# Up-projection units multiplied in pairs, in runs of 32 products

## The chip, the cores and the metric

The kernel runs on one core of one Trainium2 chip. The metric is the time of one execution on the device in microseconds; before the change the median of three runs is 2297.98 us (2297.76 to 2298.06).

The engines are called here as the profile calls them: PE (TensorE, the matrix products, with PEld for its weight loads), DVE (VectorE), ACT (ScalarE), POOL (GpSimd) and SP (the queue from which most loads are started). Each works through its own list of instructions in the order in which the program wrote it, and they wait for each other by semaphores.

## The reference, cut to what matters

Two layers, each a mixer of four kinds of attention and a feed-forward stage, on 256 positions of width 2048, in float32. The change concerns the feed-forward stage:

```python
hin = _rms_norm(x, norm_mlp_pre[l])
u = hin @ mlp_w_up[l]                      # 2048 -> 2 * 5632
u_pad = jnp.pad(u, ((0, 0), (CONV_WIDTH - 1, 0), (0, 0)))
conv = mlp_conv_b[l] + mlp_conv_w[l][0] * u_pad[:, 0:s_len]
for tap in range(1, CONV_WIDTH):
    conv = conv + mlp_conv_w[l][tap] * u_pad[:, tap:tap + s_len]
gate, up = jnp.split(conv, 2, axis=-1)
y = (jax.nn.gelu(gate, approximate=True) * up) @ mlp_w_down[l]
x = x + _rms_norm(y, norm_mlp_post[l])
```

## The kernel before, in words

**Split numbers.** A float32 weight tile `raw` is split into `hi` (rounded to the format fp32r, an ACT copy, L193) and `lo` (the rest, a DVE subtraction, L196). The activations are split once per stage into 512 columns per block of 128 channels: 256 columns high part, 256 low part (tiles `HL0` to `HL3`). A *high product* multiplies a 128x128 piece of `hi` with all 512 columns; a *low product* multiplies a piece of `lo` with the 256 high columns only. Both add into one PSUM bank, 512 columns wide.

**Units and granules.** The up-projection of a layer has 88 units of 128 output channels, even ones of the gate, odd ones of the up half. A unit needs 16 high and 16 low products (one per block of 128 input channels, `KT` = 16). Its weights come in two granules of 128x1024, which are loaded, split and used one after the other. Loads, `hi` and `lo` each have a ring of six buffers (`RAW_BUFS`, `HL_BUFS`). Units 0 to 2 are worked on in `start_block`, together with the end of the stage before; units 3 to 87 are a loop over `w_unit`.

**Order of the work.** Everything is written out in a fixed order when the program is built. `w_unit` adds two parts, one for each granule. A part is `run_gran`:

```python
fill("v")
ready(g)
emit()
used(g)
fill("pe")
```

`fill("v")` takes each *chain* that is under way one step further; `ready(g)` writes the splits of granules up to five ahead of `g` (`LOOK`), as far as their buffers' last users have been marked by `used`; `emit` writes the products. In `mm_runs` the first granule of a unit does 8 high and then 8 low products, the second 8 low and then 8 high, so that over successive units runs of 16 high (L430) and 16 low (L435) alternate.

**The chain behind a unit** is `evac(i)` in `mlp`. Its steps, one for each `fill("v")`: an ACT copy of the bank's low columns (`u`, L1504); then on DVE five operations (add the high columns L1506, multiply by the row scale L1512, and the three taps of the convolution L1515 and L1518 twice); then, for a gate unit, the GELU on ACT (`gl`, L1524), for an up unit the product with the GELU of the unit before it on DVE (`y`, L1528). When all units are done, `out_units` multiplies `y` with the down-projection (L732 to L734); it first splits each `y` into two tiles `xs`, by an ACT copy (L704) and a DVE subtraction (L705).

Of the kernel before, what the change touches and what calls it, by code (L numbers as in the profile page):

```python
# [22 lines left out]
KT = D // 128  # L23
FF = 5632
NF = FF // 128
# [111 lines left out]
def hybrid_kernel(ctx, tc, a):  # L137
    nc = tc.nc
    V, SC, TE, GP = nc.vector, nc.scalar, nc.tensor, nc.gpsimd
# [3 lines left out]
    ps = ctx.enter_context(tc.tile_pool(name="ps", bufs=1, space=bass.MemoryType.PSUM))  # L143
# [6 lines left out]
    def take(kind):  # L150
        live[kind] += 1
        assert live[kind] <= cap[kind], kind
# [5 lines left out]
    def bank():  # L158
        take("ps")
        return ps.tile([128, 512], F32, tag="ps", name="bank", bufs=8)  # L160
# [4 lines left out]
    def gran(src, c0, n, whole=False):  # L165
        return Granule(src[:, c0:c0 + n], n, whole)

    def add(f, *gs):
        work.append((f, gs))
# [46 lines left out]
    def ready(g, look=LOOK):  # L216
        prep(g.idx + look)
        assert g.idx < state["gran"]

    def used(g):  # L220
        g.uses -= 1
# [5 lines left out]
    def launch(gen, cost=0.0):  # L227
        c = Chain(gen)
        budget[0] -= cost
        if c.kind is not None:  # L230
            active.append(c)
        return c

    def may(c):
        return (all(live[k] + n <= lim[k] for k, n in c.need.items())
                and (c.cond is None or c.cond()))

    def step(c):
        c.step()
        if c.kind is None:  # L240
            active.remove(c)

    def fill(kind):
        n = 0
        for c in list(active):
            if c.kind == kind and may(c):
                step(c)
                n += 1
        return n

    def start(gain):
        budget[0] = min(budget[0] + gain, 2.0)
        n = 0
        while budget[0] > 0:
            for i in range(min(3, len(queue))):
                cost, fn, cond = queue[i]
                if cond is None or cond():
                    c = Chain(fn())
                    if not may(c):
                        continue  # L260
                    del queue[i]
                    budget[0] -= cost
                    active.append(c)
                    if c.kind == "pe":
                        step(c)
                    n += 1
                    break
            else:
                break
        return n  # L270
# [9 lines left out]
    def room(kind, n=1):  # L280
        force(lambda: live[kind] + n <= cap[kind])
# [33 lines left out]
    HL = [None] * 4  # L315
# [52 lines left out]
    def hview(k):  # L368
        return HL[k // 4][:, k % 4, :256]
# [271 lines left out]
    def w_unit(src, evac, cost):  # L641
        u = src
        gs = [gran(u, 0, 1024), gran(u, 1024, 1024)]
        box = {}

        def part(h):
            def run():
                def emit():
                    if h == 0:
                        room("ps")  # L650
                        box["a"] = bank()
                    mm_runs(box["a"], gs[h], h)
                run_gran(gs[h], 2.56, emit)
                if h == 1:
                    launch(evac(box["a"]), cost)
            return run
        add(part(0), gs[0])
        add(part(1), gs[1])

    def x_units(srcs, width, evac, cost):  # L660
        box = {}
# [196 lines left out]
    def over():  # L858
        while ends:
            ends.pop()()  # L860
# [622 lines left out]
    def mlp(l):  # L1483
        st = {}

        def begin():
            over()
            es = ExitStack()
            mp = es.enter_context(tc.tile_pool(name=f"mlp{l}", bufs=1, reuse_waits="tile"))
            st["es"], st["mp"], st["done"] = es, mp, set()  # L1490
            st["cw"] = mp.tile([128, 2 * NF + 8, 4], F32, name="cw")[:, :2 * NF]
            GP.dma_start(out=st["cw"], in_=a["conv"][l])
            st["y"] = [mp.tile([128, 256], F32, name=f"y{j}") for j in range(NF)]
            on_rows[0] = lambda: None

        def evac(i):
            j, up = divmod(i, 2)

            def f(p, first=None):
                yield "v", dict(u=1)  # L1500
                mp = st["mp"]
                take("u")
                u = mp.tile([128, 256], F32, tag="u", name="u", bufs=4)
                SC.activation(u, p[:, 256:], AF.Copy)  # L1504
                yield "v"
                V.tensor_tensor(u, u, p[:, :256], op=OP.add)  # L1506
                drop("ps")
                if first is not None:
                    add_first(u, first)
                if not scaled[0]:  # L1510
                    yield "v", {}, is_scaled
                V.tensor_tensor(u, u, r2bc, op=OP.mult)  # L1512
                cv = mp.tile([128, 256], F32, tag="cv", name="cv", bufs=5)
                w = st["cw"][:, i]
                V.tensor_scalar(cv, u, w[:, 2:3], w[:, 3:4], op0=OP.mult, op1=OP.add)  # L1515
                for tap in (1, 0):
                    n = 2 - tap
                    V.scalar_tensor_tensor(cv[:, n:], u[:, :256 - n], w[:, tap:tap + 1], cv[:, n:], op0=OP.mult,  # L1518
                                           op1=OP.add)
                drop("u")  # L1520
                if not up:
                    yield "v"
                    g = mp.tile([128, 256], F32, tag="gl", name="gl", bufs=3)
                    SC.activation(g, cv, AF.Gelu_apprx_tanh)  # L1524
                    st["g", j] = g
                else:
                    yield "v", {}, lambda: ("g", j) in st
                    V.tensor_tensor(st["y"][j], st["g", j], cv, op=OP.mult)  # L1528
                    st["done"].add(j)
            return f  # L1530

        UP = a["w_up"]
        start_block(2 * l + 1, [UP[l, i] for i in range(3)], [evac(i) for i in range(3)], mgs)
        add(begin)
        for i in range(3, 2 * NF):
            w_unit(UP[l, i], evac(i), 0.0)
        out_units(2 * l + 1, lambda p_, k2: a["w_down"][l, p_, k2], NF, lambda k: st["y"][k],
                  lambda k: k in st["done"], mgs, tail_norm(mgs) if l < DEPTH - 1 else tail_out(mgs),
                  Left(lambda: st["mp"].tile([128, 256], F32R, tag="xs", name="xs", bufs=12), "xs"),
                  lambda: st["mp"].tile([128, 1024], F32, tag="gpost", name="gpost"), l == DEPTH - 1)  # L1540

        def end():
            live["xs"] = 0
            st["es"].close()
        add(lambda: ends.append(end))
# [3 lines left out]
    for l in range(DEPTH):  # L1549
        mixer(l)  # L1550
        mlp(l)
# [95 lines left out]
```

## Time and profile before

| what | value |
|---|---|
| median of three runs | 2297.98 us |
| the profiled execution | 2297.9 us |
| its span (first to last instruction) | 2296.1 us |
| PE busy in the span | 2282.3 us, 99% |
| DVE busy | 1686.8 us, 73% |
| ACT busy | 1176.4 us, 51% |
[...]
| DMA, mean | 191 GB/s |

The time of the profiled execution is 1.8 us longer than its span; this part lies outside the instructions. Busy shares are means over stages: the up-projection of layer 0 runs from 434 to 908 us of the span, that of layer 1 from 1575 to 2049 us, each followed by its down-projection. In the timeline view a row gives start, time from the first start to the last end of a merged group, engine, line, operation, tiles, count, and in brackets how long the engine sat idle just before and what ended that.

### The profile page before, as it was taken

What the parts mean: (1) busy time and instruction counts of PE and PEld (TensorE: products, weight loads), DVE (VectorE), ACT (ScalarE), POOL (GpSimd) and SP (SyncE); (2) the same over time, 40 slices, a digit from 0 to 9 for tenths busy, and PEclk for the clock granted to TensorE, in tenths of its full rate; (3) what the DMA queues carried; (4) which work ended last, traced back from release to release, by engine and by line L of the source; (5) the groups of instructions that cost most, each with busy time, mean ns of one, the idle gap of its engine ahead of it and who ended that gap; (6) DMA issues with size and microseconds to landing.
All of it is one profiled execution on the core that took longest, in us unless ns stands there. A gap on an engine that the chain in (4) does not pass through costs nothing.

```text
span 2296.1 us, 33239 instructions
## 1 busy us (share of the span) xinstructions
PE 2282.3 (99%) x12485; PEld 1967.3 (86%) x12485; DVE 1686.8 (73%) x2901; ACT 1176.4 (51%) x1927; POOL 50.0 (2%) x71
## 2 busy tenths in 40 slices
PE   9999999999999999999999999999999999999998
PEld 7888888888888888888888888888888888888887
DVE  6757666898888888565586576568988888885655
ACT  6454555654444444455464555656444444445543
POOL 1000000100000000000010000001000000000000
PEclk9999999999999999999999999999999999999999
DMA  8764556466565565656556645564665555655663
GB/s 280 250 220 148 155 174 202 157 205 201 185 190 189 190 189 187 200 184 212 175 194 234 211 143 173 170 195 160 210 193 192 190 187 189 190 191 195 202 195 115
DMA packets 122658, 437.56 MB, mean 191 GB/s; under 512 B 13888, under 2 KB 14016, under 8 KB 122496
## 3 DMA queue, kind: packets, MB, share of 16 engines
q1 hardware_dynamic: 120384, 429.40, 57.4%
q0 software_dynamic: 1824, 5.94, 1.0%
q8 instruction: 98, 1.61, 0.3%
q14 instruction: 64, 0.52, 0.1%
q10 hardware_dynamic: 288, 0.10, 0.0%
HBM read 433.28 MB, written 2.10 MB: 190 GB/s over the span
## 4 chain that ended last, share of the span: by engine, by line
PE 96%; ACT 1%; DVE 1%; issue 1%; DMA 0%; POOL 0%; SPq 0%; DVEq 0%; POOLq 0%; ACTq 0%
PE bank L430 36%; PE bank L435 19%; PE bank L734 9%; PE bank L733 9%; PE bank L732 9%; PE bank L684 2%; PE bank L686 2%; PE bank L685 2%; PE bank L1158 1%; PE bank L1080 1%; ACT hi L193 1%; PE bank L423 1%; PE bank L467 0%; DVE x L411 0%; ACT trash L397 0%
## 5 line engine op out<-in xcount | busy, mean ns | idle before, releaser
L196 DVE TENSOR_TENSOR lo<-raw,hi 128x1024 fp32r<-128x1024 f32 (+1 forms) x786 | 948.2, 1210 | 496.3 <-ACT hi L193 495.7
L193 ACT ACTIVATE hi<-raw 128x1024 fp32r<-128x1024 f32 (+1 forms) x786 | 815.6, 1046 | 425.0 <-PE bank L734 248.3
L430 PE MATMUL bank<-HL,hi 128*128 128x512 f32 x3648 | 880.4, 392 | 0.4 <-DVE u L1506 0.4
L430 PEld LDWEIGHTS bank<-HL,hi 128*128 128x128 f32 x3648 | 668.9, 188 | 131.2 <-issue 2.8
L435 PEld LDWEIGHTS bank<-HL,lo 128*128 128x128 f32 x3648 | 469.5, 191 | 21.5 <-DVE qk L950 1.6
L435 PE MATMUL bank<-HL,lo 128*128 128x256 f32 x3648 | 480.3, 283 | 0.0
L732 PE MATMUL bank<-hi,xs 128*128 128x512 f32 x960 | 374.8, 390 | 0.0
L734 PE MATMUL bank<-hi,xs 128*128 128x512 f32 x960 | 373.6, 389 | 0.0
L733 PE MATMUL bank<-lo,xs 128*128 128x512 f32 x960 | 373.5, 389 | 0.0
L734 PEld LDWEIGHTS bank<-hi,xs 128*128 128x128 f32 x960 | 180.2, 188 | 37.3
L733 PEld LDWEIGHTS bank<-lo,xs 128*128 128x128 f32 x960 | 180.3, 188 | 37.0
L732 PEld LDWEIGHTS bank<-hi,xs 128*128 128x128 f32 x960 | 180.3, 188 | 36.9
L1518 DVE SCALAR_TENSOR_TENSOR cv<-u,cw,cv 128x255 f32<-128x255 f32 x352 | 170.0, 483 | 12.6
L1504 ACT ACTIVATE u<-bank 128x256 f32<-128x256 f32 x176 | 66.7, 381 | 202.0 <-PE bank L430 201.9
L1524 ACT ACTIVATE gl<-cv 128x256 f32<-128x256 f32 x88 | 36.8, 418 | 222.2 <-DVE cv L1518 222.2
L684 PE MATMUL bank<-hi,HL 128*128 128x512 f32 (+1 forms) x256 | 96.7, 378 | 0.5 <-ACT r2bc L501 0.5
L686 PE MATMUL bank<-hi,HL 128*128 128x512 f32 (+1 forms) x256 | 93.4, 365 | 0.0
L685 PE MATMUL bank<-lo,HL 128*128 128x512 f32 (+1 forms) x256 | 93.4, 365 | 0.0
L1512 DVE TENSOR_TENSOR u<-u,r2bc 128x256 f32<-128x256 f32 x176 | 74.9, 426 | 5.8
L1515 DVE TENSOR_SCALAR cv<-u,cw 128x256 f32<-128x256 f32 x176 | 72.6, 412 | 6.4
L1506 DVE TENSOR_TENSOR u<-u,bank 128x256 f32<-128x256 f32 x176 | 73.0, 415 | 0.0
L705 DVE TENSOR_TENSOR xs<-y,xs 128x256 fp32r<-128x256 f32 x176 | 72.1, 417 | 0.0
(227 smaller groups left out, 1402.2 us busy)
## 6 DMA issues: line engine op xcount, KB each, us to landing
raw<-in_w_up SPq DMA_DIRECT2D x352, 512.0 KB, 4.3
raw<-in_w_down SPq DMA_DIRECT2D x176, 512.0 KB, 3.7
raw<-in_w_cols SPq DMA_DIRECT2D x122, 512.0 KB, 4.4
raw<-in_w_out SPq DMA_DIRECT2D x64, 512.0 KB, 4.3
raw<-in_w_v SPq DMA_DIRECT2D x48, 512.0 KB, 4.1
raw<-in_cmp SPq DMA_DIRECT2D x32, 512.0 KB, 4.6
gpost<-in_gpost POOLq DMA_DIRECT2D x8, 512.0 KB, 6.1
raw<-in_w_x SPq DMA_DIRECT2D x8, 408.0 KB, 4.7
```

Source lines behind the costliest of these rows:

```text
L193: SC.activation(g.hi[:, c0:c0 + n], g.raw[:, c0:c0 + n], AF.Copy)
L196: eng.tensor_tensor(g.lo[:, c0:c0 + n], g.raw[:, c0:c0 + n], g.hi[:, c0:c0 + n].bitcast(F32), op=OP.subtract)
L430: TE.matmul(o, lhsT=g.hi[:, k % 8 * 128:k % 8 * 128 + 128], rhs=HL[k // 4][:, k % 4, :], start=(k == 0), stop=(k == KT - 1))
L435: TE.matmul(o[:, :256], lhsT=g.lo[:, k % 8 * 128:k % 8 * 128 + 128], rhs=hview(k), start=False, stop=False)
L684: TE.matmul(o, lhsT=h, rhs=wh, start=(K == 0), stop=False)
L685: TE.matmul(o, lhsT=h, rhs=wl, start=False, stop=False)
L686: TE.matmul(o, lhsT=lo, rhs=wh, start=False, stop=(K == KT - 1))
L732: TE.matmul(o, lhsT=h_, rhs=wh, start=(k[1] == 0), stop=False)
L733: TE.matmul(o, lhsT=h_, rhs=wl, start=False, stop=False)
L734: TE.matmul(o, lhsT=l_, rhs=wh, start=False, stop=(k[1] == nk - 1))
L1512: V.tensor_tensor(u, u, r2bc, op=OP.mult)
L1518: V.scalar_tensor_tensor(cv[:, n:], u[:, :256 - n], w[:, tap:tap + 1], cv[:, n:], op0=OP.mult, op1=OP.add)
```

## The change

A new function `w_pair` takes two units at once, with two banks, and replaces the loop over `w_unit` for units 3 to 86 of each layer (42 pairs, an up unit first and a gate unit second; unit 87 is left to `w_unit`). Its four parts write: 16 high products of the first unit and one of the second (this one clears the second bank); 16 low products of the first unit; 16 low products of the second; 15 high products of the second. With the next pair's first part this gives runs of 32 high and 32 low products. The chain behind the first unit is launched after the second part, that behind the second unit after the fourth; `used` marks granules of the first unit after the second part and of the second unit after the fourth; `ready` is called in parts 1, 2 and 3.

```diff
+    def w_pair(srcs, evacs):
+        gs = [[gran(src, 0, 1024), gran(src, 1024, 1024)] for src in srcs]
+        acc = [None, None]
+
+        def his(i, k0, k1):
+            for k in range(k0, k1):
+                g = gs[i][k // 8]
+                TE.matmul(acc[i], lhsT=g.hi[:, k % 8 * 128:k % 8 * 128 + 128], rhs=HL[k // 4][:, k % 4, :],
+                          start=(k == 0), stop=(i == 1 and k == KT - 1))
+
+        def los(i):
+            for k in range(KT):
+                g = gs[i][k // 8]
+                TE.matmul(acc[i][:, :256], lhsT=g.lo[:, k % 8 * 128:k % 8 * 128 + 128], rhs=hview(k),
+                          start=False, stop=(i == 0 and k == KT - 1))
+
+        def part(n):
+            def run():
+                fill("v")
+                if n == 0:
+                    for g in (*gs[0], gs[1][0]):
+                        ready(g)
+                    room("ps", 2)
+                    acc[:] = bank(), bank()
+                    his(0, 0, KT)
+                    his(1, 0, 1)
+                elif n == 3:
+                    his(1, 1, KT)
+                else:
+                    ready(gs[n - 1][1])
+                    los(n - 1)
+                if n % 2:
+                    for g in gs[n // 2]:
+                        used(g)
+                fill("pe")
+                start((3.6, 1.5)[n in (1, 2)])
+                if n % 2:
+                    launch(evacs[n // 2](acc[n // 2]))
+            return run
+        for n, g in enumerate((gs[0][0], gs[0][1], gs[1][0], gs[1][1])):
+            add(part(n), g)
...
-        for i in range(3, 2 * NF):
+        for i in range(3, 2 * NF - 1, 2):
+            w_pair([UP[l, i], UP[l, i + 1]], [evac(i), evac(i + 1)])
+        for i in range(2 * NF - (2 * NF - 3) % 2, 2 * NF):
             w_unit(UP[l, i], evac(i), 0.0)
```

The order of instructions before and after, at the places on which the prediction rests. Lines below the new function move by 42: L1506 becomes L1548, L1518 becomes L1560, L1524 becomes L1566, L1528 becomes L1570, L705 becomes L747, L734 becomes L776; L193 and L196 stay.

ACT in the up-projection of layer 0, before the change. `gl_4728` is the GELU of a gate unit, `cv_4702` the result of its five DVE operations; `hi_4708` and `hi_4734` are the next two granules to be split.

```order
L193 ACTIVATE hi_4679<-raw_4538 128x1024
L193 ACTIVATE hi_4708<-raw_4568 128x1024
L1524 ACTIVATE gl_4728<-cv_4702 128x256
L1504 ACTIVATE u_4730<-bank_4683 128x256
L193 ACTIVATE hi_4734<-raw_4597 128x1024
L193 ACTIVATE hi_4763<-raw_4623 128x1024
```

And now; `gl_4724` and `cv_4704` belong to the gate unit, `hi_4730` and `hi_4736` are the next two granules.

```order
L193 ACTIVATE hi_4673<-raw_4496 128x1024
L193 ACTIVATE hi_4679<-raw_4562 128x1024
L1566 ACTIVATE gl_4724<-cv_4704 128x256
L1546 ACTIVATE u_4726<-bank_4683 128x256
L193 ACTIVATE hi_4730<-raw_4568 128x1024
L193 ACTIVATE hi_4736<-raw_4619 128x1024
```

DVE at the same place before the change: the five operations of the gate unit, and the `lo` splits after them.

```order
L196 TENSOR_TENSOR lo_4680<-raw_4538,hi_4679 128x1024
L1506 TENSOR_TENSOR u_4675<-u_4675,bank_4629 128x256
L1512 TENSOR_TENSOR u_4675<-u_4675,r2bc_72 128x256
L1515 TENSOR_SCALAR cv_4702<-u_4675,cw_4377 128x256
L1518 SCALAR_TENSOR_TENSOR cv_4702<-u_4675,cw_4377,cv_4702 128x255
L1518 SCALAR_TENSOR_TENSOR cv_4702<-u_4675,cw_4377,cv_4702 128x254
L196 TENSOR_TENSOR lo_4709<-raw_4568,hi_4708 128x1024
L196 TENSOR_TENSOR lo_4735<-raw_4597,hi_4734 128x1024
L1506 TENSOR_TENSOR u_4730<-u_4730,bank_4683 128x256
```

And now.

```order
L196 TENSOR_TENSOR lo_4680<-raw_4562,hi_4679 128x1024
L1548 TENSOR_TENSOR u_4669<-u_4669,bank_4575 128x256
L1554 TENSOR_TENSOR u_4669<-u_4669,r2bc_72 128x256
L1557 TENSOR_SCALAR cv_4704<-u_4669,cw_4377 128x256
L1560 SCALAR_TENSOR_TENSOR cv_4704<-u_4669,cw_4377,cv_4704 128x255
L1560 SCALAR_TENSOR_TENSOR cv_4704<-u_4669,cw_4377,cv_4704 128x254
L196 TENSOR_TENSOR lo_4731<-raw_4568,hi_4730 128x1024
L196 TENSOR_TENSOR lo_4737<-raw_4619,hi_4736 128x1024
L1548 TENSOR_TENSOR u_4726<-u_4726,bank_4683 128x256
```

Before, the first split behind the gate unit's operations (`lo_4709`) takes a `hi` that stands in ACT's list ahead of the GELU; only the second (`lo_4735`) takes one that stands behind it. Now both (`lo_4731`, `lo_4737`) take a `hi` that stands behind the GELU, which reads the last of these operations (`cv_4704`).

DVE where the up-projection of layer 0 ends, before the change: the operations of unit 85, two splits of the down-projection's first granules, and the `xs` splits of the first two `y`. `xs_9061` is read by the third product of the down-projection.

```order
L1506 TENSOR_TENSOR u_8981<-u_8981,bank_8934 128x256
L1512 TENSOR_TENSOR u_8981<-u_8981,r2bc_72 128x256
L1515 TENSOR_SCALAR cv_9008<-u_8981,cw_4377 128x256
L1518 SCALAR_TENSOR_TENSOR cv_9008<-u_8981,cw_4377,cv_9008 128x255
L1518 SCALAR_TENSOR_TENSOR cv_9008<-u_8981,cw_4377,cv_9008 128x254
L196 TENSOR_TENSOR lo_9015<-raw_8874,hi_9014 128x1024
L1528 TENSOR_TENSOR y42_4421<-gl_8979,cv_9008 128x256
L196 TENSOR_TENSOR lo_9040<-raw_8903,hi_9039 128x1024
L705 TENSOR_TENSOR xs_9061<-y0_4379,xs_9060 128x256
L705 TENSOR_TENSOR xs_9065<-y1_4380,xs_9064 128x256
```

And now, from the third split of the down-projection's granules on; the operations of unit 85 and `y42` stand just ahead of the first row, the splits `lo_8982` and `lo_8988` of the first two granules ahead of these. `xs_9061` again goes to the third product, `xs_9111` to the 27th; `u_9029` is unit 86.

```order
L196 TENSOR_TENSOR lo_9034<-raw_8876,hi_9033 128x1024
L196 TENSOR_TENSOR lo_9040<-raw_8922,hi_9039 128x1024
L747 TENSOR_TENSOR xs_9061<-y0_4379,xs_9060 128x256
L747 TENSOR_TENSOR xs_9065<-y1_4380,xs_9064 128x256
L1548 TENSOR_TENSOR u_9029<-u_9029,bank_8935 128x256
L1554 TENSOR_TENSOR u_9029<-u_9029,r2bc_72 128x256
L1557 TENSOR_SCALAR cv_9070<-u_9029,cw_4377 128x256
L1560 SCALAR_TENSOR_TENSOR cv_9070<-u_9029,cw_4377,cv_9070 128x255
L1560 SCALAR_TENSOR_TENSOR cv_9070<-u_9029,cw_4377,cv_9070 128x254
L196 TENSOR_TENSOR lo_9077<-raw_8928,hi_9076 128x1024
L196 TENSOR_TENSOR lo_9107<-raw_8979,hi_9106 128x1024
L747 TENSOR_TENSOR xs_9111<-y2_4381,xs_9110 128x256
```

Here little has moved in the list itself: the same kinds of work stand ahead of `xs_9061`. On ACT, `hi_9106` stands behind the GELU that reads `cv_9070`.

## Rows read from the trace of the kernel before

**Rows 1.** The page: the span, the busy time of the engines with share and number of instructions, the chain that ended last, by engine, and two groups of products of 256 and of 512 columns (busy us, mean ns of one, idle before).

```profile
span 2296.1 us, 33239 instructions
PE 2282.3 (99%) x12485; PEld 1967.3 (86%) x12485; DVE 1686.8 (73%) x2901; ACT 1176.4 (51%) x1927; POOL 50.0 (2%) x71
...
PE 96%; ACT 1%; DVE 1%; issue 1%; DMA 0%; POOL 0%; SPq 0%; DVEq 0%; POOLq 0%; ACTq 0%
...
L435 PE MATMUL bank<-HL,lo 128*128 128x256 f32 x3648 | 480.3, 283 | 0.0
...
L733 PE MATMUL bank<-lo,xs 128*128 128x512 f32 x960 | 373.5, 389 | 0.0
```

**Rows 2.** What PE waited for in the up-projection of layer 0 (440 to 908 us): total, times, longest.

```profile
PE bank L430 <- DVE u L1506: 0.2, 1, 0.2
```

**Rows 3.** Busy time of the engines in a stretch of the same stage: PE, PEld, DVE, ACT, POOL, then granted clock, DMA share and GB/s.

```profile
620.00:800.00 180.00, 180.00 (x1038) 159.17 (x1037) 150.72 (x242) 84.55 (x114) 0.00 (x0) 1.00 0.59 189
```

**Rows 4.** Timeline of PE in the same stage, whole runs.

```profile
600.35 3.82 PE L430 MATMUL bank<-HL,hi 128*128 128x512 f32 x16
604.00 2.08 PE L435 MATMUL bank<-HL,lo 128*128 128x256 f32 x16
605.91 3.82 PE L430 MATMUL bank<-HL,hi 128*128 128x512 f32 x16
```

**Rows 5.** Timeline of PE cut so that only the inside of a run is seen: of a run of high products, of a run of 16 low ones, and of the late part of a run of 24 low ones in the start block (L471).

```profile
601.73 2.43 PE L430 MATMUL bank<-HL,hi 128*128 128x512 f32 x10
...
604.23 1.84 PE L435 MATMUL bank<-HL,lo 128*128 128x256 f32 x14
...
422.52 2.44 PE L471 MATMUL bank<-HL,lo 128*128 128x256 f32 x19
```

**Rows 6.** Timeline of DVE early in the stage, 456 to 480 us.

```profile
456.79 0.41 DVE L1506 TENSOR_TENSOR u<-u,bank 128x256 f32<-128x256 f32 x1
...
459.07 1.22 DVE L196 TENSOR_TENSOR lo<-raw,hi 128x1024 fp32r<-128x1024 f32 x1
460.85 1.23 DVE L196 TENSOR_TENSOR lo<-raw,hi 128x1024 fp32r<-128x1024 f32 x1 [0.57 <-ACT hi L193]
462.00 0.41 DVE L1506 TENSOR_TENSOR u<-u,bank 128x256 f32<-128x256 f32 x1
...
464.27 1.22 DVE L196 TENSOR_TENSOR lo<-raw,hi 128x1024 fp32r<-128x1024 f32 x1
465.41 0.42 DVE L1528 TENSOR_TENSOR y<-gl,cv 128x256 f32<-128x256 f32 x1
465.74 1.22 DVE L196 TENSOR_TENSOR lo<-raw,hi 128x1024 fp32r<-128x1024 f32 x1
466.88 0.41 DVE L1506 TENSOR_TENSOR u<-u,bank 128x256 f32<-128x256 f32 x1
...
469.16 1.22 DVE L196 TENSOR_TENSOR lo<-raw,hi 128x1024 fp32r<-128x1024 f32 x1
471.00 1.23 DVE L196 TENSOR_TENSOR lo<-raw,hi 128x1024 fp32r<-128x1024 f32 x1 [0.63 <-ACT hi L193]
...
479.37 1.22 DVE L196 TENSOR_TENSOR lo<-raw,hi 128x1024 fp32r<-128x1024 f32 x1
```

**Rows 7.** Timeline of ACT in the same stretch.

```profile
459.18 0.42 ACT L1524 ACTIVATE gl<-cv 128x256 f32<-128x256 f32 x1 [4.91 <-DVE cv L1518]
459.51 0.37 ACT L1504 ACTIVATE u<-bank 128x256 f32<-128x256 f32 x1
459.77 2.00 ACT L193 ACTIVATE hi<-raw 128x1024 fp32r<-128x1024 f32 x2
```

**Rows 8.** Timeline of PE at the first units of the loop in layer 0 (unit 3 begins at 434.29, unit 4 at 440.67).

```profile
434.29 1.98 PE L430 MATMUL bank<-HL,hi 128*128 128x512 f32 x8
...
440.67 2.06 PE L430 MATMUL bank<-HL,hi 128*128 128x512 f32 x8 [0.21 <-DVE u L1506]
```

**Rows 9.** Timeline of DVE later in the stage.

```profile
642.72 1.23 DVE L196 TENSOR_TENSOR lo<-raw,hi 128x1024 fp32r<-128x1024 f32 x1 [0.93 <-ACT hi L193]
```

**Rows 10.** Timeline of PE and of DVE where the up-projection of layer 0 ends: the first and the 27th product of the down-projection on PE, two `xs` splits and what follows them on DVE.

```profile
908.35 0.39 PE L732 MATMUL bank<-hi,xs 128*128 128x512 f32 x1
...
914.25 0.39 PE L734 MATMUL bank<-hi,xs 128*128 128x512 f32 x1
...
905.49 0.75 DVE L705 TENSOR_TENSOR xs<-y,xs 128x256 fp32r<-128x256 f32 x2
906.16 0.41 DVE L1506 TENSOR_TENSOR u<-u,bank 128x256 f32<-128x256 f32 x1
```

**Rows 11.** The same places in layer 1: DVE at the operations of unit 4 and the split after them, PE at the first units and at the first product of the down-projection.

```profile
1574.89 1.98 PE L430 MATMUL bank<-HL,hi 128*128 128x512 f32 x8
...
1597.41 0.41 DVE L1506 TENSOR_TENSOR u<-u,bank 128x256 f32<-128x256 f32 x1
...
2048.99 0.39 PE L732 MATMUL bank<-hi,xs 128*128 128x512 f32 x1
```

**Rows 12.** The page: the loads of the up-projection's granules, count, size and median time from issue to landing in us.

```profile
raw<-in_w_up SPq DMA_DIRECT2D x352, 512.0 KB, 4.3
```

## Prediction

> **What bounds the kernel now.** I read the page first, then PE's waits, then the timelines of PE, DVE and ACT. The page shows PE busy in 99% of the span, and 96% of the chain that ended last is PE [rows 1]. In the up-projection PE waits 0.2 us in all [rows 2], so there PE's own spacing of products is the time; DVE is busy 150.72 of 180 us, or 84% [rows 3]. A unit takes 5.565 us (605.91 to 600.35 is 5.56) [rows 4]: a run of 16 high products 3.65, a run of 16 low ones 1.91.
>
> Two things are to be seen behind this. First, DVE is close to the bound: 84% busy, in one list. Second, at the start of the stage it is behind. The split at 460.85 is preceded by 0.57 us of idling that ended with a `hi` of ACT, and the same comes at 471.00 [rows 6]. While it is behind, DVE needs 10.09 us (459.07 to 469.16) and then 10.21 us (469.16 to 479.37) for the work of two units, against 11.13 us on PE, so it catches up by about 1 us in every two units. Later it waits 0.93 us for ACT [rows 9], because it is ahead.
>
> **The change part by part.**
>
> *Fewer changes between high and low runs.* Inside a run the spacing is (2.43 - 0.39)/9 = 0.2267 us for a high product and (1.84 - 0.28)/13 = 0.1200 us for a low one [rows 5], where 0.39 and 0.28 are the duration of one product of 512 and of 256 columns [rows 1]. Sixteen of each are 5.547 us, the unit takes 5.565: a change to low runs and back costs 0.018 us. The change removes one such pair of changes for every two units, 84 in both layers: 84 x 0.018 = 1.5 us. The low spacing doesn't drift in the late part of a run of 24 ((2.44 - 0.28)/18 = 0.1200) [rows 5], so I take it to hold to 32. PE alone would then need 32 x 0.2267 + 32 x 0.1200 + 0.018 = 11.11 us for a pair.
>
> *What moves on ACT and DVE.* No operation is added or removed there. But splits are now written in twos, and in one of the two places per pair both stand behind the gate unit's five operations and behind its GELU. Before, DVE did one split (1.14 us, 464.27 to 465.41 [rows 6]) while ACT did the GELU, the copy `u` and the next `hi`; now it has nothing to do in that time, by the order quoted above. The chain itself stands in the rows: operations start 456.79, GELU 459.18, `u` 459.51, `hi` 459.77, the split that needs it 460.85 [rows 6, 7]. From the start of the operations to that split are 4.06 us, of which DVE works 2.28 (456.79 to 459.07), so 1.78 us are a hole.
>
> The work of DVE for a pair, in the new order: two splits 2.28 (twice 1.14), operations of the up unit 2.27 (462.00 to 464.27), `y` 0.33 (465.41 to 465.74), two splits 2.28, then 4.06 for the gate unit with its GELU up to the next split. The sum is 11.22 us. The other way round: before, when DVE was behind, 10.09 to 10.21, plus the 1.14 that no longer lie under the hole, is 11.23 to 11.35. I take 11.25: the first sum is of undisturbed rows, and one row in the second stretch (0.63 of idling for 0.57) shows that a few hundredths come on top.
>
> 11.25 is above PE's 11.11 and also above the 11.13 of before. So the ring DVE, ACT, DVE becomes the bound, by 0.12 us per pair; PE stops once per pair, at its 17th high product, the one that opens the second unit, because its `hi` is the one behind the GELU. Who waits behind it: all of PE's list, the 32 low and 15 high products. PE isn't part of the ring: the copies `u` of ACT read banks that were finished several us before, and the loads land in 4.3 us [rows 12] with six buffers, more than a ring early.
>
> *From where it decides.* DVE has the same work as before up to the operations of unit 4, which therefore again start at 456.79, and the `hi` behind their GELU, begun at 459.77, is again ready for its readers at 460.85 [rows 6, 7]. PE, from 434.29, with 0.81 us for the row scale's small products between units 3 and 4 (440.67 - 434.29 - 5.565) [rows 8], two pairs of 11.11 and 16 x 0.2267 = 3.63, comes there at 460.95. So already from the third pair on it is level, and there is no slack of earlier units to use up. The last pair (units 85 and 86) is 39 rings later: 460.85 + 39 x 11.25 = 899.60. From there PE has 0.23 + 32 x 0.12 + 15 x 0.2267 = 7.47, and unit 87 with 5.55: it is done at 912.6, where before the down-projection began at 908.35 [rows 10]. That is 4.3 us for one layer.
>
> *Where the stage ends.* Before, DVE was ahead here and this cost nothing; now it arrives late, and the cover is gone. DVE starts the split of unit 86's first granule at 899.6; one ring later, at 910.85, the first of the down-projection; then two splits 2.28, operations of unit 85 2.27, `y` 0.33 and two splits 2.28 bring it to 918.0; `xs` takes 0.42. The third product of the down-projection, due at 912.6 + 0.45, waits until 918.4. After it DVE has one more `xs` (0.67 for two: 905.49 to 906.16 [rows 10]), unit 86 with its GELU 4.06, a split 1.14 and an `xs` 0.42: 924.3. PE needs that at the 27th product, 918.45 + 24 x 0.2267 = 923.9, and goes on at 924.35. Before, the 27th began at 914.25 [rows 10]. From there on PE has 2.72 us (12 x 0.2267) for a granule and DVE 1.5 for its splits; nothing more is late, and nothing is won back, since PE never waited there. So a layer costs 924.35 - 914.25 = 10.1 us.
>
> *Layer 1* begins with the same distances: from PE's first unit to the operations of unit 4 22.52 us (1597.41 - 1574.89) against 22.50, and to the first product of the down-projection 474.10 against 474.06 [rows 6, 8, 10, 11]. It costs the same.
>
> *Sum.* The 1.5 us of fewer changes lie beside the ring and don't show. 2 x 10.1 = 20.2 us on the profiled execution's 2297.9 (span 2296.1 and 1.8 around it), which is the median of before within 0.1: **2318 us**.
>
> *Bounds.* The ring at 11.22 gives 40 x 0.03 x 2 = 2.4 us less, 2316; at 11.35 8 us more, 2326. If the waits at the end of the stage don't come, 2 x 4.3 = 8.6: 2306. A few tenths of DVE's lag at the start of the stage go either way.
>
> [...] The row at 460.85 shows DVE idle for 0.57 us until ACT's `hi` arrived [rows 6]; no row shows whether it could have taken a later instruction instead, since none was ready. [...]
>
> **The rivals.**
>
> 1. *Only the changes of run count.* The hole is filled or shorter by more than 0.12 us, so that a ring takes less than 11.13; then PE stays the bound, DVE goes on catching up, and the time is 2297.9 - 1.5 = 2296.4, not slower than before. It decides at the place between the gate unit's last operation and the next split. For it speaks that the margin is 1% of a ring, and that DVE in the page is at 73%; against it that each hop of the 1.78 us stands in a row of this kernel.
> 2. *The ring binds, but the end of the stage is covered*, because the first `y` are split earlier or PE's wait is shorter than my count from the list: 2306.
> 3. *Low products run faster in longer runs.* If the second 16 of a run went at 0.113 in place of 0.120, 84 x 16 x 0.007 = 9.4 us would go, with the above 2287; this needs a ring under 11.0 too. The late part of the run of 24 speaks against it.
> 4. *The ring is longer* than its rows: if every stop of PE or DVE costs 0.1 us more for the wake-up, 80 rings give 8 us, 2326, and 0.3 us give 2342.
>
> **How the numbers follow.** A difference under 0.2% (4.6 us) can't be told from no change here. My forecast, the ring with its end, has 0.66; rival 2 0.11, rival 4 beyond 2328 0.07; these are slower: 0.84. Rival 1 has 0.13, which is no change. Rival 3 has 0.03, faster. The range is that of the forecast with rival 2 and the near part of rival 4: 2305 to 2328; it leaves out about 2 in 10.
>
> **What would show it.** In the changed kernel's profile: PE's list of waits has the high product (now L667) waiting for ACT's `hi`, some 40 times per layer with 0.1 to 0.2 us each, and L776 waiting for DVE's `xs`, 5.4 and 0.4 us per layer; DVE idles 1.78 us once per pair for ACT's `hi`, also late in the stage; the distance of pairs on PE is 11.25 us, the runs 32 long with 0.2267 and 0.1200 inside. If the distance is 11.11 and PE doesn't wait, rival 1 is right and my ring is wrong.

## The result, and the profile after

| what | before | after |
|---|---|---|
| median | 2298.02 us (2297.76 to 2298.09, 4 runs) | 2329.7 us (2329.52 to 2332.07, 4 runs) |
| ratio to before, 95% interval | | 1.014 [1.0128, 1.0152] |
| span of the profiled execution | 2296.1 us | 2327.7 us |
| granted TensorE clock, mean | 0.999 | 0.997 |

The kernel is slower by 31.7 us; forecast were 20.2, with a range up to 2328. The direction and the mechanism came as forecast, the size was a third short. Two places in the trace, shown below, make up the difference: one turn of DVE's and ACT's work takes 11.36 us where 11.25 was taken, and behind the waits at the end of each up-projection PE runs for a while at a lower clock (granted were 0.52 of full speed over 3.2 us in layer 0 and 0.50 over 6 us in layer 1), for which the forecast had no term.

The page of the changed kernel: busy times, the chain that ended last by engine, and the group of weight loads for the high products of the pairs (busy us, mean ns of one, idle before).

```profile
PE 2304.2 (99%) x12485; PEld 1965.3 (84%) x12485; DVE 1688.1 (73%) x2901; ACT 1144.8 (49%) x1927; POOL 50.0 (2%) x71
...
PE 55%; DVE 31%; issue 7%; ACT 6%; POOL 0%; DVEq 0%; DMA 0%; ACTq 0%; SPq 0%; POOLq 0%
...
L667 PEld LDWEIGHTS bank<-HL,hi 128*128 128x128 f32 x2688 | 499.1, 188 | 126.8 <-ACT hi L193 29.7
```

The busy shares have hardly moved: PE 99%, DVE 73%, ACT 49%, where before they were 99, 73 and 51 [rows 1]. The chain that ended last has: PE had 96% of it, now 55%, and DVE has 31%. That the chain runs through DVE and ACT for over a third of the span, while neither is near full, points to a ring of waits; the timelines show it.

In the middle of layer 0's up-projection DVE's timeline shows one ring, from the split at 699.40 to the one at 710.75:

```profile
699.40 2.36 DVE L196 TENSOR_TENSOR lo<-raw,hi 128x1024 fp32r<-128x1024 f32 x2 [1.70 <-ACT hi L193]
701.68 0.41 DVE L1548 TENSOR_TENSOR u<-u,bank 128x256 f32<-128x256 f32 x1
...
703.04 1.00 DVE L1560 SCALAR_TENSOR_TENSOR cv<-u,cw,cv 128x255 f32<-128x255 f32 x2
704.08 0.42 DVE L1570 TENSOR_TENSOR y<-gl,cv 128x256 f32<-128x256 f32 x1
704.42 2.35 DVE L196 TENSOR_TENSOR lo<-raw,hi 128x1024 fp32r<-128x1024 f32 x2
706.69 0.41 DVE L1548 TENSOR_TENSOR u<-u,bank 128x256 f32<-128x256 f32 x1
...
708.05 1.00 DVE L1560 SCALAR_TENSOR_TENSOR cv<-u,cw,cv 128x255 f32<-128x255 f32 x2
710.75 2.36 DVE L196 TENSOR_TENSOR lo<-raw,hi 128x1024 fp32r<-128x1024 f32 x2 [1.70 <-ACT hi L193]
```

and ACT's timeline shows the other half of it:

```profile
709.08 0.42 ACT L1566 ACTIVATE gl<-cv 128x256 f32<-128x256 f32 x1 [6.60 <-DVE cv L1560]
709.41 0.36 ACT L1546 ACTIVATE u<-bank 128x256 f32<-128x256 f32 x1
709.67 2.00 ACT L193 ACTIVATE hi<-raw 128x1024 fp32r<-128x1024 f32 x2
```

DVE finishes the gate unit's operations at 709.05 and idles 1.70 us, until ACT has done GELU, `u` and the first `hi`; ACT before that has idled 6.60 us until DVE had done those operations. Each waits for the other, once per pair. Term by term the ring is two splits 2.28, the up unit's operations up to `y` 2.40 (701.68 to 704.08), `y` 0.34, two splits 2.27, and 4.06 from the gate unit's operations to the next split. That is 11.35.

PE's timeline in the same stage, three rows of whole runs, answers to [rows 4]:

```profile
612.76 7.69 PE L667 MATMUL bank<-HL,hi 128*128 128x512 f32 x32
620.29 4.00 PE L673 MATMUL bank<-HL,lo 128*128 128x256 f32 x32
624.12 7.68 PE L667 MATMUL bank<-HL,hi 128*128 128x512 f32 x32
```

A pair takes 11.36 us on PE too (624.12 - 612.76). Undisturbed runs of 32 high products last 7.44 us (an experiment below, in which PE is the bound again, has them); here it is 7.69. PE's own list of waits for this stage doesn't have this stop, because a product is 0.39 us long in the profile [rows 1] and even here the next starts before its end (the one at 619.95, 0.36 us behind the start at 619.59), so that PE reads as busy all the time (180.00 of 180 us in the first row of the windows below). The list of waits of the weight loads (PEld) has it (layer 0, 440 to 908 us: total, times, longest):

```profile
PEld bank L667 <- ACT hi L193: 14.9, 39, 0.4
```

These are 39 stops of 0.38 us. They cost 0.24 us each, the difference between 11.355 and the 11.11 of PE alone; the other 0.14 us of an idle weight load, an estimate from these two numbers, lie under products that are still running.

Where the stage ends, on PE: the last run of the up-projection, the first products of the down-projection (the first row of L774, then the third product, L776) and the 27th (last row), which answer to [rows 10].

```profile
915.10 2.00 PE L430 MATMUL bank<-HL,hi 128*128 128x512 f32 x8
918.54 0.50 PE L774 MATMUL bank<-hi,xs 128*128 128x512 f32 x1 [1.44 <-ACT xs L746]
...
922.87 0.80 PE L776 MATMUL bank<-hi,xs 128*128 128x512 f32 x1 [3.60 <-DVE xs L747]
923.47 0.63 PE L774 MATMUL bank<-hi,xs 128*128 128x512 f32 x1
...
925.60 0.53 PE L776 MATMUL bank<-hi,xs 128*128 128x512 f32 x1
925.97 0.39 PE L774 MATMUL bank<-hi,xs 128*128 128x512 f32 x1
...
929.82 0.39 PE L776 MATMUL bank<-hi,xs 128*128 128x512 f32 x1
```

The two waits for `xs` are 1.44 and 3.60 us. Behind the second of them a product lasts 0.63 us instead of 0.39. The granted clock is lower there. The windows view (columns as in [rows 3], the granted clock behind POOL's), of a stretch in the middle of the stage and of two at its end:

```profile
620.00:800.00 180.00, 180.00 (x1018) 155.24 (x1019) 149.21 (x240) 74.35 (x110) 0.00 (x0) 1.00 0.56 185
...
916.90:922.80 5.90, 0.93 (x3) 0.30 (x2) 5.72 (x11) 2.84 (x5) 0.00 (x0) 0.97 0.63 197
922.80:926.00 3.20, 3.13 (x8) 2.51 (x9) 3.06 (x8) 0.54 (x2) 0.00 (x0) 0.52 0.74 283
```

In the second row PE was busy 0.93 of 5.90 us, and in the third the mean clock was 0.52 of full speed. The products from 923.47 to 925.60 are 0.43 us apart, where they are 0.2267 apart later.

From one layer to the other nothing is won back. The 27th product stands 929.82 - 914.25 = 15.57 us behind the kernel before in layer 0. In layer 1 it stands at 2086.50:

```profile
2079.17 0.80 PE L776 MATMUL bank<-hi,xs 128*128 128x512 f32 x1 [3.60 <-DVE xs L747]
...
2086.50 0.39 PE L776 MATMUL bank<-hi,xs 128*128 128x512 f32 x1
```

In the kernel before, that product is at 2054.89, 5.90 after the first [rows 11], so the difference is 31.61 us there, as large as that of the spans (31.6). In the changed kernel's layer 1 the clock was low already while PE stood still: 0.50 from 2077 to 2083 us.

### The profile page after: what moved, and what is told of

Its sections match the earlier page's. It is cut to its first block, busy times and chain, and to the rows that moved or that the text cites. A ratio compares the mean times of both kernels' runs of the same rounds, so it can differ in the third digit from the quotient of the medians.

```text
span 2327.7 us, 33399 instructions
## 1 busy us (share of the span) xinstructions
PE 2304.2 (99%) x12485; PEld 1965.3 (84%) x12485; DVE 1688.1 (73%) x2901; ACT 1144.8 (49%) x1927; POOL 50.0 (2%) x71
## 4 chain that ended last, share of the span: by engine, by line
PE 55%; DVE 31%; issue 7%; ACT 6%; POOL 0%; DVEq 0%; DMA 0%; ACTq 0%; SPq 0%; POOLq 0%
DVE lo L196 13%; PE bank L776 9%; PE bank L774 9%; PE bank L775 9%; PE bank L430 9%; DVE cv L1560 7%; PE bank L435 5%; ACT hi L193 4%; DVE u L1554 3%; DVE cv L1557 3%; DVE u L1548 3%; PE bank L726 2%; PE bank L728 2%; PE bank L727 2%; ACT u L1546 1%
## 5 line engine op out<-in xcount | busy, mean ns | idle before, releaser
L196 DVE TENSOR_TENSOR lo<-raw,hi 128x1024 fp32r<-128x1024 f32 (+1 forms) x786 | 933.9, 1210 | 523.4 <-ACT hi L193 523.0
L193 ACT ACTIVATE hi<-raw 128x1024 fp32r<-128x1024 f32 (+1 forms) x786 | 799.8, 1045 | 349.5 <-PE bank L776 248.3
L667 PE MATMUL bank<-HL,hi 128*128 128x512 f32 x2688 | 643.6, 393 | 0.0
L667 PEld LDWEIGHTS bank<-HL,hi 128*128 128x128 f32 x2688 | 499.1, 188 | 126.8 <-ACT hi L193 29.7
L776 PE MATMUL bank<-hi,xs 128*128 128x512 f32 x960 | 375.3, 391 | 7.2 <-DVE xs L747 7.2
L774 PE MATMUL bank<-hi,xs 128*128 128x512 f32 x960 | 376.2, 392 | 2.9 <-ACT xs L746 2.9
L673 PEld LDWEIGHTS bank<-HL,lo 128*128 128x128 f32 x2688 | 334.2, 191 | 4.1
L673 PE MATMUL bank<-HL,lo 128*128 128x256 f32 x2688 | 336.6, 283 | 0.0
L1566 ACT ACTIVATE gl<-cv 128x256 f32<-128x256 f32 x88 | 36.8, 418 | 561.7 <-DVE cv L1560 561.7
L776 PEld LDWEIGHTS bank<-hi,xs 128*128 128x128 f32 x960 | 181.1, 189 | 45.9 <-DVE xs L747 8.1
L774 PEld LDWEIGHTS bank<-hi,xs 128*128 128x128 f32 x960 | 181.1, 189 | 40.3 <-ACT xs L746 3.7
L1560 DVE SCALAR_TENSOR_TENSOR cv<-u,cw,cv 128x255 f32<-128x255 f32 x352 | 170.2, 484 | 12.5
L435 PEld LDWEIGHTS bank<-HL,lo 128*128 128x128 f32 x960 | 124.9, 190 | 8.4 <-DVE qk L992 1.6
L435 PE MATMUL bank<-HL,lo 128*128 128x256 f32 x960 | 131.6, 285 | 0.0
```

Of the source, the lines that this page charges most:

```text
L193: SC.activation(g.hi[:, c0:c0 + n], g.raw[:, c0:c0 + n], AF.Copy)
L196: eng.tensor_tensor(g.lo[:, c0:c0 + n], g.raw[:, c0:c0 + n], g.hi[:, c0:c0 + n].bitcast(F32), op=OP.subtract)
L435: TE.matmul(o[:, :256], lhsT=g.lo[:, k % 8 * 128:k % 8 * 128 + 128], rhs=hview(k), start=False, stop=False)
L667: TE.matmul(acc[i], lhsT=g.hi[:, k % 8 * 128:k % 8 * 128 + 128], rhs=HL[k // 4][:, k % 4, :], start=(k == 0), stop=(i == 1 and k == KT - 1))
L673: TE.matmul(acc[i][:, :256], lhsT=g.lo[:, k % 8 * 128:k % 8 * 128 + 128], rhs=hview(k), start=False, stop=(i == 0 and k == KT - 1))
L774: TE.matmul(o, lhsT=h_, rhs=wh, start=(k[1] == 0), stop=False)
```

## The experiments

The questions were three. Is it the order of the splits or the run length that costs the time? Which operation makes the ring a tenth longer than its rows before? And what does the stage's end cost by itself? In the diffs "before" and "after" are the two kernels above. Ratios are to the kernel before, on the same chip.

### Run length alone taken back

The lists of ACT and DVE stay as after; only the products of a pair are written in runs of 16.

```diff
-                          start=(k == 0), stop=(i == 1 and k == KT - 1))
+                          start=(k == 0), stop=False)
...
-                          start=False, stop=(i == 0 and k == KT - 1))
+                          start=False, stop=(k == KT - 1))
...
                     his(0, 0, KT)
-                    his(1, 0, 1)
                 elif n == 3:
-                    his(1, 1, KT)
+                    los(1)
                 else:
                     ready(gs[n - 1][1])
-                    los(n - 1)
+                    (los, lambda i: his(i, 0, KT))[n - 1](n - 1)
```

> The changed kernel with the same lists on ACT and DVE (splits, chains, order), but PE's products of a pair in the order of before: 16 high and 16 low of the first unit, then 16 high and 16 low of the second. Ring theory: the ring of 11.36 us holds as before, 2328 to 2331 us. Rival, the run length is what costs: back to 2298 us.

Measured: 2330.72 us (2329.65 to 2331.45), ratio 1.0139 [1.0122, 1.0156]. PE's timeline:

```profile
703.20 2.08 PE L673 MATMUL bank<-HL,lo 128*128 128x256 f32 x16
705.11 3.82 PE L667 MATMUL bank<-HL,hi 128*128 128x512 f32 x16
...
710.79 3.96 PE L667 MATMUL bank<-HL,hi 128*128 128x512 f32 x16
```

The runs are 16 long and the loss is the same. DVE's ring is 11.35 us here too (from 699.42 to 710.77). One high run of each pair is 3.96 us long instead of 3.82, so a part of PE's stop stands in it. The loss doesn't need the long runs.

### Split order alone, in the kernel before

Here the products are those of the kernel before; only the splits of a unit's two granules are both written in its first part (with 0 in place of `LOOK` the second part writes none ahead).

```diff
-    def run_gran(g, us, emit):
+    def run_gran(g, us, emit, look=LOOK):
         fill("v")
-        ready(g)
+        ready(g, look)
...
-    def w_unit(src, evac, cost):
+    def w_unit(src, evac, cost, twos=False):
...
-                run_gran(gs[h], 2.56, emit)
+                run_gran(gs[h], 2.56, emit, 0 if twos and h else LOOK)
...
-            w_unit(UP[l, i], evac(i), 0.0)
+            w_unit(UP[l, i], evac(i), 0.0, i < 2 * NF - 1)
```

> The kernel before with one move: in the loop over units splits are written only in the first part of a unit, two at a time, so that both stand behind the GELU on ACT; PE's list keeps its 8 high, 16 low, 16 high as before and no pair is made. Ring theory: DVE's list is that of the changed kernel, the ring is 11.36 us, 2328 to 2331 us. Rival, the pairs on PE cost the time: 2298 us.

Measured: 2330.49 us (2329.23 to 2331.87), ratio 1.014 [1.0125, 1.0155]. DVE's timeline:

```profile
699.65 2.36 DVE L196 TENSOR_TENSOR lo<-raw,hi 128x1024 fp32r<-128x1024 f32 x2 [1.70 <-ACT hi L193]
...
711.01 2.36 DVE L196 TENSOR_TENSOR lo<-raw,hi 128x1024 fp32r<-128x1024 f32 x2 [1.71 <-ACT hi L193]
```

The same hole, the same distance of 11.36, the same loss, in a kernel that has none of the pairs. Writing the splits in twos is enough to cause it.

### Splits ahead of the gate unit's GELU

After, with the splits that the third part of a pair writes, those of the next granules, written before the chains take their step; on ACT both `hi` then stand ahead of the GELU. The operations are the same. The call is the one that this part makes a few lines later anyway.

```diff
         def part(n):
             def run():
+                if n == 2:
+                    ready(gs[1][1])
                 fill("v")
```

> The changed kernel with one move: in the third part of a pair the splits of the next granules are written ahead of the chains' steps, so that on ACT the two hi stand ahead of the GELU; PE's runs of 32 stay as they are. Ring theory: the hole of 1.7 us on DVE goes, the ring falls from 11.36 to about 9.7 us, PE (11.11 us per pair) is the bound again, the waits at the end of the stage go too: 2298.0 - 1.5 = 2296.5 us (2295.5 to 2298). Rival, the long runs themselves cost the time (two open banks, 32 weight loads in a row): stays near 2330 us.

Measured: 2296.83 us (2296.31 to 2299.09), ratio 0.9995 [0.9986, 1.0004]. The whole loss is gone. DVE's timeline, and behind it ACT's:

```profile
703.43 2.36 DVE L196 TENSOR_TENSOR lo<-raw,hi 128x1024 fp32r<-128x1024 f32 x2 [1.46 <-ACT hi L193]
...
707.07 1.00 DVE L1562 SCALAR_TENSOR_TENSOR cv<-u,cw,cv 128x255 f32<-128x255 f32 x2
707.99 2.35 DVE L196 TENSOR_TENSOR lo<-raw,hi 128x1024 fp32r<-128x1024 f32 x2
```

```profile
702.07 0.38 ACT L1548 ACTIVATE u<-bank 128x256 f32<-128x256 f32 x1 [4.38 <-PE bank L667]
```

The splits now follow the gate unit's operations without idling (707.99). DVE still idles 1.46 us per pair, nearly as long as after; but the chain behind that hole is another: the `hi` it waits for stands on ACT behind a `u` that waits 4.38 us for PE's bank. DVE waits because it is ahead of PE, which is the bound again, so this hole costs nothing. The runs of PE are 7.44 and 4.00 long again:

```profile
709.55 7.44 PE L667 MATMUL bank<-HL,hi 128*128 128x512 f32 x32
716.84 4.00 PE L673 MATMUL bank<-HL,lo 128*128 128x256 f32 x32
```

A pair takes 11.12 us (720.67 - 709.55 on PE), where PE alone was worked out at 11.11.

### One of the two splits ahead

After, with one split only, that of the next granule, written before the chain's step; the other follows it as before.

```diff
+                if n == 2:
+                    prep(state["gran"])
                 fill("v")
```

> The changed kernel with one of the two splits of a pair's third part written ahead of the chains' steps (ahead of the GELU) and one behind, as before the change. Ring theory: DVE has 1.14 us of split to do while the GELU, u and the other hi run; the hole shrinks from 1.7 to about 0.57 us, the ring to about 10.2 us while DVE is behind, under PE's 11.11: DVE catches up, PE is the bound: 2296.5 us (2295.5 to 2298). Rival, it is enough that any split stands behind the GELU (the lists of ACT and DVE stay coupled once per pair): a ring of 11.1 or more, 2300 to 2325 us.

Measured: 2296.48 us (2296.28 to 2296.95), ratio 0.9993 [0.9983, 1.0003]. DVE's timeline:

```profile
708.43 1.22 DVE L196 TENSOR_TENSOR lo<-raw,hi 128x1024 fp32r<-128x1024 f32 x1
710.22 1.23 DVE L196 TENSOR_TENSOR lo<-raw,hi 128x1024 fp32r<-128x1024 f32 x1 [0.57 <-ACT hi L193]
```

This is the pattern of [rows 6] at 459.07 to 460.85: a split lies under the GELU, and the hole that is left is 0.57 us. With 1.14 us of work in the hole a ring would take 11.35 - 1.14 = 10.2 us, far below PE's 11.11. This ring can't be seen in the trace, where PE sets the pace; the time shows that it takes *both* splits behind the GELU for the ring to bind.

### The product `y` a step later

After, with an empty step ahead of `y` in the chain of an up unit, so that on DVE the two splits stand between its operand's last operation and it.

```diff
                 else:
+                    yield "v"
                     yield "v", {}, lambda: ("g", j) in st
                     V.tensor_tensor(st["y"][j], st["g", j], cv, op=OP.mult)
```

> The changed kernel with the product y written one step later, behind two splits in place of directly behind the operation whose result it reads. Ring theory with the wait of y for its own operand (0.12 us) as the missing part of my sum: the ring falls from 11.36 to 11.24 us, 40 rings in each of two layers: 2329.7 - 9.4 = 2320 us (2318 to 2323). Rival, the missing tenth lies in the hops between DVE and ACT: 2328 to 2330 us.

Measured: 2320.41 us (2319.57 to 2322.28), ratio 1.0097 [1.0082, 1.0112], 9.3 us less than after. DVE's timeline:

```profile
700.90 1.00 DVE L1560 SCALAR_TENSOR_TENSOR cv<-u,cw,cv 128x255 f32<-128x255 f32 x2
701.82 2.35 DVE L196 TENSOR_TENSOR lo<-raw,hi 128x1024 fp32r<-128x1024 f32 x2
704.09 0.42 DVE L1571 TENSOR_TENSOR y<-gl,cv 128x256 f32<-128x256 f32 x1
...
708.49 2.36 DVE L196 TENSOR_TENSOR lo<-raw,hi 128x1024 fp32r<-128x1024 f32 x2 [1.71 <-ACT hi L193]
...
719.72 2.36 DVE L196 TENSOR_TENSOR lo<-raw,hi 128x1024 fp32r<-128x1024 f32 x2 [1.71 <-ACT hi L193]
```

The ring is 11.23 (719.72 - 708.49), 0.12 less, with the same operations. Read the starts: here a split that doesn't read the result of the operation in front starts 0.08 us before that one's end (701.82 against 700.90 + 1.00); after, `y` stood directly behind the operation whose result it reads and started 0.04 behind its end (704.08 against 703.04 + 1.00). 80 rings of 0.12 are 9.6 us. That is the missing tenth; the hole behind the GELU is 1.71 us as after, so the hops between DVE and ACT don't have it.

### First `xs` splits earlier

After, with the first `xs` splits of the down-projection written before the third part of the last pair rather than before the second part of unit 87.

```diff
-        work.insert(len(work) - 1, (pre, ()))
+        work.insert(len(work) - (4 if nk == NF else 1), (pre, ()))
```

> The changed kernel with the first two xs splits written before the third part of the last pair of the up-projection, so that they don't stand behind four splits of the down-projection. Theory A, the end of the stage is late because DVE as a whole is behind: only the 0.67 us of work that now fits into DVE's last hole behind the GELU is saved in each layer, and PE waits later for a split in place of the xs: 2328 to 2329.7 us. Theory B, the order at the end alone makes the wait: the 5 us of waiting per layer go, 2318 to 2321 us.

Measured: 2329.56 us (2329.34 to 2329.95), ratio 1.0138 [1.0121, 1.0155]: nothing gained. PE's timeline:

```profile
922.07 0.39 PE L776 MATMUL bank<-hi,xs 128*128 128x512 f32 x1
926.70 0.79 PE L774 MATMUL bank<-hi,xs 128*128 128x512 f32 x1 [4.24 <-ACT xs L746]
...
928.58 0.63 PE L774 MATMUL bank<-hi,xs 128*128 128x512 f32 x1
```

The first 24 products run without a stop; then PE waits 4.24 us for the `xs` of the next two `y`, which stand behind the same ring on ACT and DVE, and products are 0.63 us long again. The wait was moved, not removed: what is late is the list as a whole, not one `xs`. Theory A had the time right, but it expected PE to wait for a split there, not for an `xs`.

### The wait filled with products

After, with 14 more products between the second and the third of the down-projection, into a bank that is cleared before it is used; nothing is left out of the computation.

```diff
                 TE.matmul(o, lhsT=h_, rhs=wl, start=False, stop=False)
+                if nk == NF and k == (0, 0) and (t, c) == (0, 0):
+                    for _ in range(14):
+                        TE.matmul(accs["a"][1][1], lhsT=h_, rhs=wh, start=True, stop=True)
```

> The changed kernel with 14 products more in each layer, between the second and the third product of the down-projection, into a bank that is cleared afterwards: they fill 3.2 us of the 3.6 us in which PE waits for xs there. If the seven slow products behind that wait (about 0.42 us apart in place of 0.23) come from PE having stood still, they go back to 0.23 us and 1.4 us per layer are saved: 2329.7 - 2.8 = 2327 us (2326 to 2328.5). If they come from something else (the xs or the banks arriving one by one), they stay slow: 2329.5 to 2330.

Measured: 2327.32 us (2326.37 to 2327.77), ratio 1.0127 [1.0112, 1.0142]: with 28 products *more* it is 2.4 us faster than after. The same stretch in windows, and PE's timeline of the third, fourth and 27th product:

```profile
922.80:926.00 3.20, 3.20 (x16) 2.60 (x15) 2.91 (x5) 1.29 (x3) 0.00 (x0) 1.00 0.55 205
```

```profile
922.12 0.50 PE L779 MATMUL bank<-hi,xs 128*128 128x512 f32 x1 [0.38 <-DVE xs L747]
922.46 0.40 PE L774 MATMUL bank<-hi,xs 128*128 128x512 f32 x1
...
928.00 0.50 PE L779 MATMUL bank<-hi,xs 128*128 128x512 f32 x1
```

The clock is 1.00 where it was 0.52. From the third to the 27th product it takes 5.88 us here in both layers (928.00 - 922.12 in layer 0), after 6.95 in layer 0 and 7.33 in layer 1: the low clock cost 1.07 and 1.45, together 2.5 us.

## Why the prediction was right or wrong

*Fewer changes between runs.* Right in size. With the ring out of the way a pair takes 11.12 where 11.11 was worked out. In layer 0 the low runs of PE that begin at 459.27 and 904.60 in the kernel before are 40 pairs of units apart, 445.33 us; those at 450.12 and 894.65 in the kernel with the splits ahead of the GELU, also 40 pairs apart, 444.53 us. That is 0.020 us less per pair, 1.7 us for 84, where 1.5 was forecast. The times alone don't show it: the two kernels whose splits are mended come 1.1 and 1.4 us below the kernel before, but both intervals hold 1.

*The ring.* Right in kind: it binds, for the reason given, and two experiments from opposite sides (split order put into the kernel before; splits moved in the kernel after) show that the twos behind the GELU make it and that the pairs on PE don't. That DVE doesn't take an operation ahead of one that waits is in the trace: the up unit's `u` was ready at 709.77 (709.41 and 0.36), its operations stood two splits further down, and DVE idled until 710.75. The kernel before has it too, where the prediction took no later instruction to be ready: `u` was ready at 459.88 (459.51 and 0.37 [rows 7]), its operations stood one split further down, and DVE idled until 460.85 [rows 6].

*The ring's length* is the step that failed first. The sum had 2.27 for the up unit's operations, read in the kernel before from 462.00 to 464.27 [rows 6]. But what stood behind them there was a split, which doesn't read their result; in the new order `y` stands there, which does. The same five operations then take 2.40, the ring 11.35 instead of the 11.25 taken. The kernel before showed this price already, within the same five operations:

```profile
462.44 0.42 DVE L1512 TENSOR_TENSOR u<-u,r2bc 128x256 f32<-128x256 f32 x1
...
463.35 1.00 DVE L1518 SCALAR_TENSOR_TENSOR cv<-u,cw,cv 128x255 f32<-128x255 f32 x2
```

The operation at 462.44 reads the result of the one at 462.00 and starts 0.03 us behind its end (462.00 + 0.41); the split at 464.27 starts 0.08 us ahead of the end of the last one (463.35 + 1.00). The bounds of the prediction had a ring of 11.35 too (2326 us), but taken from a turn with a longer hole (0.63), that is for another cause.

*From where it decides*, and how often, was right: the third pair's split is at 460.94, forecast 460.85, and the one 39 rings later at 903.75, forecast 899.60. These rows of the changed kernel's DVE, with the first `xs` of the down-projection, forecast to start at 918.0:

```profile
460.94 2.36 DVE L196 TENSOR_TENSOR lo<-raw,hi 128x1024 fp32r<-128x1024 f32 x2 [1.71 <-ACT hi L193]
...
903.75 2.36 DVE L196 TENSOR_TENSOR lo<-raw,hi 128x1024 fp32r<-128x1024 f32 x2 [1.71 <-ACT hi L193]
...
922.40 0.75 DVE L747 TENSOR_TENSOR xs<-y,xs 128x256 fp32r<-128x256 f32 x2
```

(903.75 - 460.94)/39 is 11.354. The 0.104 over the forecast make 4.1 us by the last pair and 4.4 by the first `xs`.

*Where the stage ends.* Right in the wait: 3.60 and 1.44 us for `xs`, together 5.0, where 5.4 were expected at the third product alone. That the first product would wait for ACT was not foreseen, but its wait lies inside the same time. The 0.4 us at the 27th don't show, because the slow products had used them up. What the step lacked is the clock, the second step that failed: it had 24 x 0.2267 behind the third product, all at full pace and without a reason given, and the first of them ran at the lower clock. That is the second cause, 1.07 and 1.45 us beyond the 0.4 us wait. The trace of the kernel before has a sign of it at its very end: PE's last product ends at 2288.51 (the first row), and the granted clock is 1.00 up to 2290 and 0.50 from 2292 on.

```profile
2288.12 0.39 PE L734 MATMUL bank<-hi,xs 128*128 128x512 f32 x1
...
2288.50:2290.00 1.50, 0.01 (x1) 0.00 (x0) 0.67 (x2) 0.69 (x2) 0.38 (x1) 1.00 0.45 172
...
2292.00:2294.00 2.00, 0.00 (x0) 0.00 (x0) 0.95 (x2) 0.00 (x0) 0.00 (x0) 0.50 1.01 381
```

With a wait of 5.4 us in the forecast, a low clock behind it belonged among the rivals.

*Layer 1 costs the same.* Nearly: 15.6 and 16.0 us; 9 products were slow in place of 7.

*The sum*, corrected: 2 x 10.1 as forecast, 2 x 4.4 to 4.5 for the ring (the experiment on `y`: 9.3), 2.5 for the clock (the filled wait: 2.4). That is 31.5 to 31.7, and measured were 31.7. Each of the two steps alone would have left the time inside the stated range (2318 + 8.9 or 2318 + 2.5); together they pass its end. That the sum meets the time to a tenth is in part luck, since the clock's price isn't fixed: from the third to the 27th product it takes 7.93 and 7.14 us in the kernel with `y` a step later, 8.21 and 7.99 in the one with runs of 16, for 6.95 and 7.33 here.

*The rivals.* The first (only the run count) fell, and its price was right: 2296.4 against the 2296.83 and 2296.48 of the kernels in which the hole has work or is gone. The second (the end covered) fell; even with `xs` written earlier nothing was covered. The third (faster low products) fell: the low run of 32 lasts 4.00, as 0.28 + 31 x 0.12 gives. The fourth (a longer ring) came true, but not by wake-ups at stops: the 4.06 us from the gate unit's operations to the next split came out as their rows said. The forecast's hole of 1.78 us is the same as the 1.70 of the profile: it counts from where a split would have started, 0.08 us ahead of the end of the operation in front.

*What would show it.* The waits of L667 for ACT's `hi` were forecast for PE's list of waits, some 40 per layer with 0.1 to 0.2 us each; they stand in that of the weight loads, 39 with 0.38 us each in layer 0. The distance of pairs was 11.36 for 11.25, and the wait at the 27th product didn't come.

## What to carry to other kernels

An engine that is busy 73% of the span can bind, here DVE with ACT: before putting work in twos, follow the list of each engine around the loop and add up one turn, holes included, against the pace of the engine that is meant to bound. A duration read from start to start contains who stands behind (here 2.27 us with a split behind, 2.40 with `y`); when the order changes, look for every operation that now stands directly behind the one whose result it reads. And where a change is to make PE wait for some microseconds, the products behind the wait may run at a lower clock (here 0.52 and 0.50, for 1.07 and 1.45 us), so the wait isn't the whole price.

## What the runs showed of the hardware

- After a stretch in which PE was busy 0.93 of 5.90 us, the granted clock was 0.52 over the next 3.2 us. When it fell and how long it stayed low differed: in layer 0 it was 0.97 from 922.0 to 922.5, 0.50 from there to 925.0 and 1.00 from 926.0; in layer 1 it was 0.50 already from 2077.0, before PE went on, to 2083.0. Filling the wait with 14 products kept it at 1.00 (918.0 to 926.0). What exactly makes it fall wasn't tried.
- On DVE an operation of 256 columns that reads the result of the one in front started 0.04 us after that one's end, a split that doesn't 0.08 us before it: 0.12 us for standing next to one's operand.
